# Output product of a hybrid decoder step on one Trainium2 core: squares summed apart, attention's rows tile by tile, no sums on GpSimd

## The chip, the cores and the metric

One of the eight cores of a Trainium2 chip (trn2) runs the whole program. The metric is device time in microseconds (us) of one execution. The engines are named PE (TensorE, matmuls; PEld is its weight load), DVE (VectorE), ACT (ScalarE), POOL (GpSimd) and SP (SyncE, which issues the weight DMAs).

## What is computed

Two layers of a decoder trunk, for 256 prompt tokens and 8 sample tokens together (T = 264 columns), in float32. Each layer is a SwiGLU block, a mixer and a second SwiGLU block, each behind an RMS norm:

```python
yp = yp + 0.5 * swiglu(rmsnorm(yp, norm_ffn1[l]), ...)
h = rmsnorm(yp, norm_mix[l])
b_g, u, qn, qp, ckv, kpe = mixer_project(h, ...)      # ckv = rmsnorm(kv_c), kpe = rope(k_pe)
conv_y = b_g * short_conv(u_hist, conv_w[l], SEQ)     # 512 wide
attn_o = prompt_mla(qn, qp, ckv, kpe, w_kv_b[l])      # 8 heads x 64 = 512 wide
merged = concatenate([rmsnorm(conv_y, gn_conv), rmsnorm(attn_o, gn_attn)])
yp = yp + merged @ w_o[l]                             # the output product, 1024 x 1024
yp = yp + 0.5 * swiglu(rmsnorm(yp, norm_ffn2[l]), ...)
```

## The kernel before, in words

Activations lie feature by feature: eight tiles of 128 features by 264 tokens. A weight arrives as a 1 MB chunk and is split into a high and a low part: ACT rounds it (line 231), DVE subtracts (line 233, "lo"), each in two halves of 128x512. A product is then three matmuls (lines 250 to 252: high by high, high by low, low by high). Five units (a column tile of 128 features each) fit in the split buffers, so the next unit is split when PE has finished an old one.

The code is traced in an order, and the scheduler then orders each engine's queue by its own model of readiness; each engine works through its queue strictly in that order. `behind()` puts the DVE half of a split behind the instruction that `after[0]` names at that moment. The mixer weaves three generators (`main`: the convolution's products; `prompt`: attention of the prompt; `sample`: attention of the sample) by the string ORDER.

`main` (lines 870 to 916): for each of the four convolution tiles, z is computed on DVE (line 901), ACT makes its scaled high part (905) and its square (907 or 910), DVE its low part (911) and the sum of squares in ssB (913). `h_out` (687) adds the squares of attention's rows into ssA on POOL (704). `latent` normalises the latents (578), rounds them on ACT (580), subtracts on DVE (581) and rotates the key on POOL (596 to 598).

The output product (933 to 987): `o_stats` (933) sums ssA and ssB over the features by a transposing reduction on DVE (316) and a matmul with `fold` (317, "sums"), then a reciprocal root in small DVE instructions (302 to 309, 939 to 945). `a_spread` (947) spreads the factor over rows (321) and, for each of attention's four tiles, multiplies (953, DVE), rounds (954, ACT) and subtracts (955, DVE); these are the tiles `qg` in the trace. `o_part` gives the matmuls of one k tile: k = 0 to 3 are the convolution's rows (`r` in the trace), k = 4 to 7 attention's. The first four output tiles are built side by side in four PSUM banks, k outermost; the last four one after another. `o_finish` scales a finished bank (963), adds it to y (964), lets a weight unit be split (`done`), and calls `finish_y`: the next block's high and low parts `xg` (331 ACT, 332 DVE), the square (336, 339 ACT) and its sum, on POOL for seven of eight tiles (343). The second SwiGLU then opens with four units at once, each one k tile behind the one before (`kouter`, lag 1), and takes the four PSUM banks over as `o_finish` frees them.

The scratch rows `wtile` share one tag, "w", with four buffers: the softmax rows p of a head (665), their transposed form (684), and the spread factors. Each stays taken from its first writer to its last reader. A softmax of head h can start when a buffer is free; `h_out` (694) frees two when it has used a pair of heads.

At the program's start the squares of y are summed at lines 1011 to 1022, tiles 1 to 3 on POOL, 5 to 7 on DVE.

Of the kernel before, what the change touches and what calls it, by code (L numbers as in the profile page):

```python
# [7 lines left out]
F32 = mybir.dt.float32  # L8
# [10 lines left out]
SEQ = 256  # L19
# [89 lines left out]
def trunk_kernel(ctx: ExitStack, tc: tile.TileContext, a: dict, o: dict):  # L109
# [199 lines left out]
        after[0] = V.scalar_tensor_tensor(r, t, 5.0, r, ALU.add, ALU.mult).ins  # L309
        return r  # L310

    def sums(ps, ss, c0=0):


        q = small(NBLK, tag="sums")
        V.tensor_reduce(q, ss.rearrange("p (c j) -> p c j", j=32), AX.X, ALU.add, apply_transpose=True)
        PE.matmul(ps[:, c0:c0 + NBLK], fold, q, start=True, stop=True)

    def over_rows(out, r):

# [8 lines left out]
    def finish_y(kt, g, split=True, square=True, pool=False, last=False):  # L329
        if split:  # L330
            S.activation(xg["h"][:, kt], y[:, kt], AF.Copy, scale=g)  # L331
            V.scalar_tensor_tensor(xg["l"][:, kt], y[:, kt], g, xg["h"][:, kt].bitcast(F32), ALU.mult, ALU.subtract)  # L332
        if not square:
            return
        if kt == 0:
            S.activation(ssA[:, :T], y[:, kt], AF.Square, scale=D ** -0.5)
        else:
            sq = t264()
            S.activation(sq[:, :T], y[:, kt], AF.Square, scale=D ** -0.5)
            if kt == KT - 1 and last:  # L340
                nrm["sq"] = sq
                return
            (G if pool else V).tensor_tensor(ssA[:, :T], ssA[:, :T], sq[:, :T], ALU.add)

    nrm = {}

# [149 lines left out]
    def mixer(l):  # L496
# [62 lines left out]
        kgs = [mt([P, 4, SEQ], f"kg{g}") for g in range(2)]  # L559
        qgs = [mt([P, 4, T], f"qg{g}") for g in range(2)]  # L560
        zh, zl = [], []
        Sc = Rb


# [9 lines left out]
        def latent():  # L574
            s2 = st["s2"]
            Rk = wtile(TP)
            over_rows(Rk, s2[:, 0:NBLK])
            V.tensor_tensor(ckvf, kvg, Rk[:, :T], ALU.mult)
            ckh, ckl = r264(), r264()
            S.activation(ckh, ckvf, AF.Copy)  # L580
            after[0] = V.tensor_tensor(ckl, ckvf, ckh.bitcast(F32), ALU.subtract).ins

            sel = small(8, tag="qsel")
# [9 lines left out]
            kp2 = t264()  # L593
            with behind():
                V.stream_shuffle(kp2[64:96, :T], kp1[64:96, :T], SWAP)
            G.tensor_tensor(kp1[64:96, :T], kp1[64:96, :T], cos[64:96], ALU.mult)
            G.tensor_tensor(kp2[64:96, :T], kp2[64:96, :T], sin[64:96], ALU.mult)
            G.tensor_tensor(kpf[64:96], kp1[64:96, :T], kp2[64:96, :T], ALU.add)

        def values():  # L600
            wh, wl = [w[:, 0, NH * NOPE:] for w in st["wkv"]]
# [85 lines left out]
        def h_out(t):  # L687
# [11 lines left out]
            if t == 0:  # L699
                S.activation(ssA[:, 0:SEQ], ps[:, 0:256], AF.Square, scale=CD ** -0.5)  # L700
            else:
                sq = t264()[:, :SEQ]
                S.activation(sq, ps[:, 0:256], AF.Square, scale=CD ** -0.5)
                G.tensor_tensor(ssA[:, 0:SEQ], ssA[:, 0:SEQ], sq, ALU.add)

        def prompt():
            low_rank()
# [162 lines left out]
        def main():  # L870
            cs, us = {}, {}
            for c in (0, 2):
                for part in (1, 2, 0):
                    for j in range(2):
# [24 lines left out]
                        else:  # L899
# [2 lines left out]
                            done()  # L902
                            g = gain("gn_conv", 4 * l, ct)
                            h, lo = r264(), r264()
                            S.activation(h, z, AF.Copy, scale=g)
                            if ct == 0:
                                S.activation(ssB[:, :T], z, AF.Square, scale=CD ** -0.5)
                            else:
                                sq = t264()[:, :T]
                                S.activation(sq, z, AF.Square, scale=CD ** -0.5)  # L910
                            V.scalar_tensor_tensor(lo, z, g, h.bitcast(F32), ALU.mult, ALU.subtract)
                            if ct:
                                V.tensor_tensor(ssB[:, :T], ssB[:, :T], sq, ALU.add)
                            zh.append(h)
                            zl.append(lo)
                        yield
# [16 lines left out]
        def o_stats():  # L933

            ps = bank("x")
            sums(ps, ssA)
            sums(ps, ssB, NBLK)
            v = small(2 * NBLK, tag="v2")
            V.tensor_scalar(v[:, 0:NBLK], ps[:, 0:NBLK], EPS, None, ALU.add)
            V.tensor_tensor(v[:, NBLK:], ps[:, NBLK:2 * NBLK], ev, ALU.add)  # L940
# [6 lines left out]
        def a_spread():  # L947
            fa = st["fa"]
            Ra = wtile(TP)
            over_rows(Ra, fa)  # L950
            for t in range(CT):
                f = t264()[:, :T]
                V.scalar_tensor_tensor(f, st["attn"][:, t], gain("gn_attn", 4 * l, t), Ra[:, :T], ALU.mult, ALU.mult)
                S.activation(mg[0][:, t], f, AF.Copy)
                V.tensor_tensor(mg[1][:, t], f, mg[0][:, t].bitcast(F32), ALU.subtract)

        def o_part(ps, w, k):
            xh, xl = (zh[k], zl[k]) if k < CT else (mg[0][:, k - CT], mg[1][:, k - CT])
# [10 lines left out]
        open_xg()  # L969
        us = [take() for _ in range(4)]  # L970
        pss = [bank("mm") for _ in range(4)]
        for k in range(KT):
            for w, ps in zip(us, pss):
                o_part(ps, w, k)
            if k == 2:
                a_spread()
            if k == 5:
                c_spread()
            if k == 5:
                c_store()  # L980
        for m in range(4):
            o_finish(m, pss[m])
        for m in range(4, KT):
            w, ps = take(), bank("mm")
# [27 lines left out]
    for kt in range(KT):  # L1012
        acc = hi if kt >= 4 else ssA[:, :T]
        if kt % 4 == 0:
            S.activation(acc, y[:, kt], AF.Square, scale=D ** -0.5)
        else:
            sq = t264()[:, :T]
            S.activation(sq, y[:, kt], AF.Square, scale=D ** -0.5)
            (V if kt >= 4 else G).tensor_tensor(acc, acc, sq, ALU.add)
        if kt == 3:  # L1020
            split_unit()
    V.tensor_tensor(ssA[:, :T], ssA[:, :T], hi, ALU.add)
# [129 lines left out]
```

## Time and profile before

| what | value |
| --- | --- |
| three runs | 1040.4, 1041.53, 1047.66 us; median 1041.53 |
| the profiled execution | 1033.67 us, its span 1031.9 us |
| mean granted TensorE clock of it | 0.995 |
| PE, DVE, ACT, POOL busy | 97%, 74%, 52%, 9% of the span |

The page's busy times are shares of the span; "idle before <-X" in a timeline row is how long the engine had waited before that instruction and whose work ended the wait. Starts of consecutive instructions on one engine may lie closer than their durations, since they are pipelined.

### The profile page before, as it was taken

The page shows a single profiled execution, that of the slowest core. Times are in us where ns is not written, and L with a number is a line of the kernel's source. Part 1 is how long each engine was busy: PE and PEld are TensorE (multiplying, and loading weights), DVE is VectorE, ACT ScalarE, POOL GpSimd, SP SyncE. Part 2 cuts the span into 40 slices and gives each one's busy share as a digit, 9 for nine tenths or more (in the row PEclk, how much of TensorE's full clock was granted, in tenths as well). Part 3 has the DMA queues.
Part 4 walks back from the last instruction along what each step waited for, and adds up shares of the span by engine and source line. Part 5 has one row for each costly group of instructions (what it writes and reads, how often), then busy time and mean ns, then how long its engine had stood idle before and what let it go on. Part 6 is the DMA issues. An engine that isn't in the chain of part 4 may idle for free.

```text
span 1031.9 us, 21616 instructions
## 1 busy us (share of the span) xinstructions
PE 1001.6 (97%) x8666; PEld 970.5 (94%) x8666; DVE 764.0 (74%) x1753; ACT 535.9 (52%) x1167; POOL 93.9 (9%) x135
## 2 busy tenths in 40 slices
PE   8999999999999999999999999999999899999996
PEld 7999999988788999999999999999878899999996
DVE  6988866689859877756688888566996897777452
ACT  6555445448636555545555555454674555555441
POOL 2110100030402000000001111000322100000000
PEclk9999999999999999999999999999999999999998
DMA  8867665535614755555566667454554265555531
GB/s 276 276 221 242 217 199 193 173 109 194 247 42 164 240 169 191 177 164 188 180 213 232 219 226 230 159 179 154 170 192 178 93 208 191 189 178 174 165 113 43
DMA packets 170787, 190.03 MB, mean 184 GB/s; under 512 B 3936, under 2 KB 163712, under 8 KB 170688
## 3 DMA queue, kind: packets, MB, share of 16 engines
q1 hardware_dynamic: 164048, 167.53, 49.7%
q0 software_dynamic: 5776, 19.49, 5.4%
q10 hardware_dynamic: 864, 1.64, 0.5%
q8 instruction: 68, 1.11, 0.4%
q14 instruction: 31, 0.25, 0.1%
HBM read 187.19 MB, written 1.49 MB: 183 GB/s over the span
## 4 chain that ended last, share of the span: by engine, by line
PE 85%; DVE 10%; ACT 3%; issue 1%; DMA 1%; ACTq 0%; SPq 0%; DVEq 0%
PE mm L250 27%; PE mm L252 27%; PE mm L251 26%; DVE lo L233 4%; PE x L779 1%; DVE y L964 1%; ACT hi L231 1%; DVE xg L332 1%; PE x L830 1%; DMA raw<-in_w_ffn_gate_dram 1%; PE x L694 1%; PE x L681 1%; DVE t L963 1%; ACT qg L635 0%; PE s L658 0%
## 5 line engine op out<-in xcount | busy, mean ns | idle before, releaser
L231 ACT ACTIVATE hi<-raw 128x512 fp32r<-128x512 f32 (+1 forms) x648 | 366.2, 612 | 367.3 <-PE mm L251 245.4
L233 DVE TENSOR_TENSOR lo<-raw,hi 128x512 fp32r<-128x512 f32 (+1 forms) x648 | 417.2, 677 | 112.2 <-ACT hi L231 102.7
L252 PE MATMUL mm<-xg,lo 128*128 128x264 f32 x1648 | 468.0, 284 | 7.1 <-DVE lo L233 7.0
L250 PE MATMUL mm<-xg,hi 128*128 128x264 f32 x1648 | 471.2, 286 | 2.4 <-DVE t L963 1.7
L251 PE MATMUL mm<-xg,hi 128*128 128x264 f32 x1648 | 467.4, 284 | 0.0
L252 PEld LDWEIGHTS mm<-xg,lo 128*128 128x128 f32 x1648 | 308.8, 188 | 10.6 <-DVE lo L233 9.6
L250 PEld LDWEIGHTS mm<-xg,hi 128*128 128x128 f32 x1648 | 310.5, 188 | 5.1 <-ACT hi L231 3.6
L251 PEld LDWEIGHTS mm<-xg,hi 128*128 128x128 f32 x1648 | 310.6, 188 | 0.2
L250 PE MATMUL mm<-act,hi 128*128 128x264 f32 x704 | 200.4, 285 | 0.0
L252 PE MATMUL mm<-act,lo 128*128 128x264 f32 x704 | 199.7, 284 | 0.0
L251 PE MATMUL mm<-act,hi 128*128 128x264 f32 x704 | 199.2, 283 | 0.0
L250 PEld LDWEIGHTS mm<-act,hi 128*128 128x128 f32 x704 | 132.3, 188 | 0.2 <-ACT t L1040 0.2
L252 PEld LDWEIGHTS mm<-act,lo 128*128 128x128 f32 x704 | 132.5, 188 | 0.0
L251 PEld LDWEIGHTS mm<-act,hi 128*128 128x128 f32 x704 | 132.4, 188 | 0.0
L464 POOL DMA_INDIRECT nat<-in_cache_ckv_dram,idx x32 | 33.4, 1044 | 445.7 <-DVE lo L233 189.7
L403 DVE TENSOR_TENSOR t<-mm,t 128x264 f32<-128x264 f32 x88 | 37.6, 427 | 40.1 <-PE mm L252 39.6
L394 DVE TENSOR_TENSOR t<-mm,Rw 128x264 f32<-128x264 f32 x88 | 37.6, 428 | 38.4 <-PE mm L252 38.4
L331 ACT ACTIVATE xg<-y,gains 128x264 fp32r<-128x264 f32 x48 | 24.1, 514 | 29.8 <-DVE y L449 19.1
L397 ACT ACTIVATE t<-t 128x264 f32<-128x264 f32 x88 | 36.3, 412 | 4.4 <-DVE t L394 4.3
L399 DVE SCALAR_TENSOR_TENSOR t<-t,t 128x264 f32<-128x264 f32 x88 | 37.6, 428 | 1.1 <-ACT t L397 1.1
L406 DVE TENSOR_TENSOR act<-t,act 128x264 fp32r<-128x264 f32 x88 | 37.7, 428 | 0.0
L405 ACT ACTIVATE act<-t 128x264 fp32r<-128x264 f32 x88 | 36.0, 409 | 0.7 <-DVE t L403 0.6
(230 smaller groups left out, 808.3 us busy)
## 6 DMA issues: line engine op xcount, KB each, us to landing
raw<-in_w_ffn_up_dram SPq DMA_DIRECT2D x44, 1024.0 KB, 5.2
raw<-in_w_ffn_gate_dram SPq DMA_DIRECT2D x43, 1024.0 KB, 5.2
raw<-in_w_ffn_down_dram SPq DMA_DIRECT2D x32, 1024.0 KB, 5.3
raw<-in_w_in_dram SPq DMA_DIRECT2D x14, 1024.0 KB, 5.4
raw<-in_w_ffn_down_dram SPq DMA_DIRECT2D x16, 768.0 KB, 4.6
raw<-in_w_o_dram SPq DMA_DIRECT2D x8, 1024.0 KB, 5.2
raw<-in_w_q_dram SPq DMA_DIRECT2D x2, 768.0 KB, 5.0
raw<-in_w_in_dram SPq DMA_DIRECT2D x2, 640.0 KB, 4.0
```

The source lines that it names most:

```text
L231: S.activation(h[:, k, f], raw[:, k, lo:hi][:, :, f], AF.Copy)
L233: V.tensor_tensor(r[:, k, f], raw[:, k, lo:hi][:, :, f], h[:, k, f].bitcast(F32), ALU.subtract)
L250: PE.matmul(ps, wh, xh, start=start, stop=False)
L251: PE.matmul(ps, wh, xl, start=False, stop=False)
L252: return PE.matmul(ps, wl, xh, start=False, stop=stop)
L394: V.tensor_tensor(g1, ps[:, :T], Rb, ALU.mult)
L397: S.activation(th, g1, AF.Tanh, scale=0.5)
L399: evac[0] = V.scalar_tensor_tensor(a1[m], th, 1.0, g1, ALU.add, ALU.mult).ins
L403: V.tensor_tensor(t, ps[:, :T], a1.pop(m), ALU.mult)
L405: S.activation(ah[:, m], t, AF.Copy)
L406: evac[0] = V.tensor_tensor(al[:, m], t, ah[:, m].bitcast(F32), ALU.subtract).ins
L464: G.indirect_dma_start(dst, None, src, bass.IndirectOffsetOnAxis(ap=idx[l][:, b:b + 1], axis=0))
```

## The change

In the order of the code: `sums` can continue an accumulation in PSUM. All sums of squares go to DVE (finish_y, h_out, the start). The latents are rounded by DVE straight from the product that makes them, no longer by ACT from the stored tile, and the rotated key is made by DVE. The last convolution tile's square is made by DVE into a tile of its own, `sqB`, taken from the "w" buffers early in the mixer, and summed by a matmul of its own; its low part is traced after that. `a_spread` multiplies all four tiles before it subtracts, and sets `after[0]`. The output product's first four tiles take the convolution's rows side by side and then attention's rows tile by tile.

```diff
-    def sums(ps, ss, c0=0):
+    def sums(ps, ss, c0=0, start=True, stop=True):
-        PE.matmul(ps[:, c0:c0 + NBLK], fold, q, start=True, stop=True)
+        PE.matmul(ps[:, c0:c0 + NBLK], fold, q, start=start, stop=stop)
...
-            (G if pool else V).tensor_tensor(ssA[:, :T], ssA[:, :T], sq[:, :T], ALU.add)
+            V.tensor_tensor(ssA[:, :T], ssA[:, :T], sq[:, :T], ALU.add)
...
+        sqB = wtile(TP)
+        G.memset(sqB[:, T:TP], 0.0)
...
+            ckh, ckl = r264(), r264()
+            V.tensor_tensor(ckh, kvg, Rk[:, :T], ALU.mult)
             V.tensor_tensor(ckvf, kvg, Rk[:, :T], ALU.mult)
-            ckh, ckl = r264(), r264()
-            S.activation(ckh, ckvf, AF.Copy)
...
-            G.tensor_tensor(kp1[64:96, :T], kp1[64:96, :T], cos[64:96], ALU.mult)
-            G.tensor_tensor(kp2[64:96, :T], kp2[64:96, :T], sin[64:96], ALU.mult)
-            G.tensor_tensor(kpf[64:96], kp1[64:96, :T], kp2[64:96, :T], ALU.add)
+                V.tensor_tensor(kp1[64:96, :T], kp1[64:96, :T], cos[64:96], ALU.mult)
+                V.tensor_tensor(kp2[64:96, :T], kp2[64:96, :T], sin[64:96], ALU.mult)
+                V.tensor_tensor(kpf[64:96], kp1[64:96, :T], kp2[64:96, :T], ALU.add)
...
-                G.tensor_tensor(ssA[:, 0:SEQ], ssA[:, 0:SEQ], sq, ALU.add)
+                V.tensor_tensor(ssA[:, 0:SEQ], ssA[:, 0:SEQ], sq, ALU.add)
...
+                            if ct < CT - 1:
...
+                            else:
+                                V.scalar_tensor_tensor(sqB[:, :T], z, 1.0 / CD, z, ALU.mult, ALU.mult)
+                                S.activation(h, z, AF.Copy, scale=g)
+                                st["lo"] = lo, z, g, h
...
             sums(ps, ssA)
-            sums(ps, ssB, NBLK)
+            sums(ps, sqB, NBLK, start=True, stop=False)
+            lo, z, g, h = st["lo"]
+            V.scalar_tensor_tensor(lo, z, g, h.bitcast(F32), ALU.mult, ALU.subtract)
+            sums(ps, ssB, NBLK, start=False, stop=True)
...
+            fs = []
             for t in range(CT):
-                f = t264()[:, :T]
-                V.scalar_tensor_tensor(f, st["attn"][:, t], gain("gn_attn", 4 * l, t), Ra[:, :T], ALU.mult, ALU.mult)
-                S.activation(mg[0][:, t], f, AF.Copy)
-                V.tensor_tensor(mg[1][:, t], f, mg[0][:, t].bitcast(F32), ALU.subtract)
+                fs.append(t264()[:, :T])
+                after[0] = V.scalar_tensor_tensor(fs[t], st["attn"][:, t], gain("gn_attn", 4 * l, t), Ra[:, :T], ALU.mult, ALU.mult).ins
+                S.activation(mg[0][:, t], fs[t], AF.Copy)
+            for t in range(CT):
+                V.tensor_tensor(mg[1][:, t], fs[t], mg[0][:, t].bitcast(F32), ALU.subtract)
...
-        for k in range(KT):
+        for k in range(CT):
             for w, ps in zip(us, pss):
                 o_part(ps, w, k)
-            if k == 2:
+            if k == 1:
                 a_spread()
-            if k == 5:
                 c_spread()
-            if k == 5:
                 c_store()
         for m in range(4):
+            for k in range(CT, KT):
+                o_part(pss[m], us[m], k)
             o_finish(m, pss[m])
...
-            (V if kt >= 4 else G).tensor_tensor(acc, acc, sq, ALU.add)
+            V.tensor_tensor(acc, acc, sq, ALU.add)
```

## Rows read from the trace of the kernel before

**Rows 1.** The page: the chain that ended last, shares of the span by engine.
```profile
PE 85%; DVE 10%; ACT 3%; issue 1%; DMA 1%; ACTq 0%; SPq 0%; DVEq 0%
```

**Rows 2.** Windows: stretch, its us, busy of each engine (instructions), granted clock, DMA.
```profile
260.00:290.00 30.00, 29.82 (x512) 22.48 (x508) 23.27 (x88) 18.13 (x58) 12.21 (x17) 1.00 0.60 213
...
300.40:308.10 7.70, 7.63 (x48) 7.48 (x49) 3.08 (x9) 2.21 (x6) 0.00 (x0) 0.78 0.01 2
...
795.20:803.70 8.50, 6.59 (x54) 6.27 (x52) 6.44 (x23) 2.30 (x6) 0.00 (x0) 1.00 0.35 118
803.70:809.90 6.20, 6.14 (x48) 5.99 (x49) 3.10 (x9) 2.24 (x6) 0.00 (x0) 1.00 0.01 3
809.90:821.60 11.70, 11.70 (x98) 11.70 (x97) 11.70 (x23) 10.29 (x23) 3.73 (x4) 1.00 0.53 170
821.60:836.50 14.90, 12.95 (x100) 12.19 (x99) 13.57 (x34) 6.78 (x15) 1.82 (x3) 1.00 0.45 149
```

**Rows 3.** Timeline of PE, layer 1: start, us, line, tiles, idle before.
```profile
798.09 0.28 PE L251 MATMUL mm<-r,hi 128*128 128x264 f32 x1
...
798.52 0.37 PE L252 MATMUL mm<-r,lo 128*128 128x264 f32 x1
...
801.50 0.29 PE L252 MATMUL mm<-r,lo 128*128 128x264 f32 x1
803.75 0.75 PE L250 MATMUL mm<-qg,hi 128*128 128x264 f32 x4 [1.96 <-ACT qg L954]
...
824.55 0.36 PE L250 MATMUL mm<-xg,hi 128*128 128x264 f32 x1 [0.83 <-DVE t L963]
...
828.25 0.51 PE L252 MATMUL mm<-xg,lo 128*128 128x264 f32 x2 [1.09 <-DVE lo L233]
```

**Rows 4.** Timeline of DVE, layer 1, from the last convolution tile to attention's tiles.
```profile
795.39 0.43 DVE L901 TENSOR_TENSOR t<-t,mm 128x264 f32<-128x264 f32 x1 [0.23 <-PE mm L252]
796.86 0.49 DVE L911 SCALAR_TENSOR_TENSOR r<-t,gains,r 128x264 fp32r<-128x264 f32 x1 [1.04 <-ACT r L905]
...
797.73 0.48 DVE L316 TRANSPOSE_TENSOR_REDUCE sm<-ssB 128x9 f32<-128x288 f32 x1
798.70 0.17 DVE L939 TENSOR_SCALAR sm<-x 128x9 f32<-128x9 f32 x1 [0.48 <-PE x L317]
...
801.20 0.68 DVE L233 TENSOR_TENSOR lo<-raw,hi 128x512 fp32r<-128x512 f32 x1
...
802.76 1.29 DVE L953 SCALAR_TENSOR_TENSOR t<-attn,gains,w 128x264 f32<-128x264 f32 x3
```

**Rows 5.** Timeline, layer 1: additions to y on DVE, and one sum on POOL.
```profile
809.73 0.77 DVE L964 TENSOR_TENSOR y<-y,t 128x264 f32<-128x264 f32 x2
...
815.29 0.99 DVE L964 TENSOR_TENSOR y<-y,t 128x264 f32<-128x264 f32 x1
...
815.03 0.96 POOL L343 TENSOR_TENSOR ssA<-ssA,t 128x264 f32<-128x264 f32 x1 [1.90 <-ACT t L339]
```

**Rows 6.** Timeline of DVE, the program's start.
```profile
13.88 2.31 DVE L233 TENSOR_TENSOR lo<-raw,hi 128x512 fp32r<-128x512 f32 x2 [0.86 <-ACT hi L231]
```

**Rows 7.** Timeline, layer 1: the latents on DVE, the rotated key on POOL.
```profile
725.03 0.43 DVE L581 TENSOR_TENSOR r<-ckvf,r 128x264 fp32r<-128x264 f32 x1 [0.80 <-ACT r L580]
...
725.98 3.05 DVE L233 TENSOR_TENSOR lo<-raw,hi 128x512 fp32r<-128x512 f32 x4
...
727.32 1.16 POOL L596 TENSOR_TENSOR t<-t,con 32x264 f32<-32x264 f32 x1
```

**Rows 8.** Timeline, layer 1: softmax rows and their use in attention of the prompt.
```profile
770.17 0.35 DVE L665 CUSTOM_DVE_ANT_0 w<-s,tri,sm 128x128 f32<-128x128 f32 x1 [0.15 <-PE x L694]
...
775.01 0.55 DVE L684 COPY w<-x 128x384 f32<-128x384 f32 x1
...
786.28 0.87 PE L694 MATMUL x<-w,v 128*64 128x256 f32 x8
...
789.12 0.87 PE L694 MATMUL x<-w,v 128*64 128x256 f32 x8
```

More of the change, by code (lines that the diff above doesn't have):

```diff
@@ L904, in main @@
                             h, lo = r264(), r264()
-                            S.activation(h, z, AF.Copy, scale=g)
-                            if ct == 0:
-                                S.activation(ssB[:, :T], z, AF.Square, scale=CD ** -0.5)
-                            else:
[L909 to L913, printed above, removed]
+                            if ct < CT - 1:
+                                S.activation(h, z, AF.Copy, scale=g)
+                                if ct == 0:
+                                    S.activation(ssB[:, :T], z, AF.Square, scale=CD ** -0.5)
+                                else:
+                                    sq = t264()[:, :T]
+                                    S.activation(sq, z, AF.Square, scale=CD ** -0.5)
+                                V.scalar_tensor_tensor(lo, z, g, h.bitcast(F32), ALU.mult, ALU.subtract)
+                                if ct:
+                                    V.tensor_tensor(ssB[:, :T], ssB[:, :T], sq, ALU.add)
+                            else:
+                                V.scalar_tensor_tensor(sqB[:, :T], z, 1.0 / CD, z, ALU.mult, ALU.mult)
+                                S.activation(h, z, AF.Copy, scale=g)
+                                st["lo"] = lo, z, g, h
                             zh.append(h)
@@ L936, in o_stats @@
             sums(ps, ssA)
-            sums(ps, ssB, NBLK)
+            sums(ps, sqB, NBLK, start=True, stop=False)
+            lo, z, g, h = st["lo"]
+            V.scalar_tensor_tensor(lo, z, g, h.bitcast(F32), ALU.mult, ALU.subtract)
+            sums(ps, ssB, NBLK, start=False, stop=True)
             v = small(2 * NBLK, tag="v2")
```

## The prediction

> **What bounds the kernel now.** I began with the chain of work that ended last [rows 1]: 85% of it is PE, 10% VectorE. So the kernel is bound by matmuls, and an edit can only give back places where PE waits or runs slowly. The windows over the stages [rows 2] show where those are. The reader should compare instruction counts with lengths. Where PE is fed, 98 matmuls take 11.70 us, 0.119 each (809.9 to 821.6). The stretch before it has 48 in 6.20 us, nearly as dense. But the same 48 in layer 0 (300.4 to 308.1) take 7.70 us, and there the granted clock reads 0.78 instead of 1.00. The opening of the second SwiGLU has 100 in 14.90 us, where 100 x 0.119 = 11.9 would do: 3.0 us of waits. The convolution's rows of the output product take 8.50 us for 54 instructions. Attention (260 to 290) keeps PE busy for 29.82 of 30 us: nothing to win there, only to lose. Each of these stretches occurs twice, once per layer, with equal lengths but for the clock.
>
> The timeline of PE [rows 3] shows the waits themselves: the last convolution row starts at 801.50, attention's first at 803.75, behind ACT's rounding of its rows; then two waits at 824.55 and 828.25, behind VectorE's evacuation of a bank and behind the low part of a weight. VectorE explains the latter [rows 2]: it works 3.10 of 6.20 us while four banks fill side by side, then 11.70 of 11.70 us, and the backlog still stands when the SwiGLU opens.
>
> **Term 1, the wait before attention's rows.** Before: 803.75 - 801.50 = 2.25, less one spacing of 0.12, so 2.1 us per layer. On VectorE [rows 4] z starts at 795.39, waits for ACT (1.04 us before the low part at 796.86), the sum goes into ssB, the reduction starts at 797.73 and the first result from PE is used at 798.70, 0.97 later. New: z 0.43, square 0.49 (a like form at 796.86), then again 0.97: 795.39 + 1.89 = 797.3, 1.4 us earlier, as long as the older sums are reduced before z or behind sqB. If the low part and the other reduction come in between, 0.97 - 0.48 = 0.5 us remains. Then from 801.20 to 802.76 two weight splits (0.68 the first) and the spreading stand in front of attention's tiles; the new `after[0]` puts the splits behind: 1.56 less the spreading's 0.48 (a like form at 797.73), another 1.1 us. Attention's first tile thus starts at about 802.76 - 2.5 = 800.3, its rounded rows reach PE 0.99 later (802.76 to 803.75), at 801.3, before PE is through. The low part now comes after four multiplications (1.29 / 3 = 0.43 each): 800.3 + 1.7 + 0.4 = 802.4. PE has the third sums to do first; one costs the step from 798.09 to 798.52 less 0.12, so 0.31 [rows 3], and four high products bring it to about 802.4. I leave 0.2 of waiting and 0.3 of sums: gain 1.6 us per layer. Bounds: 0 (nothing shorter comes through) to 2.0.
>
> **Term 2, the opening of the SwiGLU.** Output tiles finished one by one let VectorE begin after 12 matmuls (1.4 us) instead of after nearly all 48: most of its 3.1 idle us are used [rows 2]. Against that, two splits (1.1 us) now lie behind attention's tiles, where they used to lie ahead. The sums on POOL: six per layer. Two additions on VectorE take 0.77 us together, 0.39 each; one that meets a POOL sum takes 0.99 [rows 5], 0.6 more. Six moved sums cost 6 x 0.39 = 2.3, and free about 6 x 0.5 to 0.6 = 3.0 to 3.6 us (not each meets an addition in full). So VectorE gains roughly 3.1 - 1.1 + 0.7 = 2.7 us or a little more on PE, against 3.0 us of waits. What will be late next is the chain of the last unit: its buffers come free only with the last output tile, and it has to be split by ACT and VectorE before 828.25's matmul can run. I leave 0.6 us: gain 2.4 per layer. Bounds: 0, if VectorE's queue is as late as before, to 3.0. No queue is held by a moved sum unless ACT's square is late. ACT is busy 10.3 of 11.7 us there [rows 2], so it can be, and the evacuations would queue behind; that is in the 0.6.
>
> [...]
>
> **Term 3, the clock.** [...] With the wait gone I take 1.5 as gained. Bounds: -1.5 (a new wait drops it elsewhere) to 1.5. [...]
>
> **Term 4, the start.** Two splits take 2.31 us beside POOL's three sums [rows 6], where one split alone takes 0.68 [rows 4]: 0.9 us or more is lost. Three additions on VectorE cost 1.2, and 0.86 of idle time lies ahead of them. Gain 0.5; bounds -0.5 to 1.0.
>
> **Term 5, the latents.** VectorE waited 0.80 us for ACT's rounding at 725.03 [rows 7]; one product of 0.43 replaces it, 0.4 earlier. Three instructions for the rotated key come onto VectorE, some 1.3 us, ahead of the splits that PE needs; but the four splits there took 3.05 us, 0.76 each instead of at most 0.68 [rows 4], beside POOL's version. That is -0.4 + 1.3 - 0.3 = 0.6 later at first, which I expect the later splits, free of POOL, to give back: 0. Bounds: 0.8 us per layer either way. The three sums of `h_out` (1.2 us of VectorE, 23.27 of 30 us busy in that stretch) I cost at nothing; attention's PE queue hides them.
>
> **Term 6, the buffer.** sqB takes one of four "w" buffers from its clearing on POOL, early in the mixer, until the statistics. Attention's softmax rows have three left. Already before, a softmax waited for a buffer: at 770.17, for the output of the first pair [rows 8]. With three, the second head of each pair has to wait too. The last pair came 2.8 us behind the third (786.28 to 789.12) since head 7 had been prepared. Without that it needs a whole chain: 770.17 to 775.01, plus the copy of 0.55 and the product's 0.87, 6.3 us; so attention would end 3.5 us later per layer. Its sums were reduced before z came, and the convolution's chain still follows, so most of that is covered: I take 0.5 per layer. Bounds: 0 to 3.5.
>
> **The sum**, against the profiled execution's 1033.67 us: 2 x 1.6 + 2 x 2.4 + 1.5 + 0.5 + 0 - 2 x 0.5 = 9.0 us. That gives 1024.7. The median of the three runs lies 7.9 us above the profiled execution, so I take the difference off the median: 1041.5 - 9.0 = 1032.5 us.
>
> **The rivals.** A is the forecast: 0.42, with 6 to 10.4 us gained.
>
> B: the buffer costs nothing and both waits go almost wholly: 2 x 1.8 + 2 x 2.8 + 1.5 + 0.6 = 11.3, 1030.2 us. For it: attention's chain has slack; four rounds of 6.3 us from 770.2 would be done at the same time as now. Against: the last unit's split. 0.34.
>
> C: the change does not do what it says in the queue. The scheduler already mixes the four banks (four high products at 803.75 in one row [rows 3]), and VectorE has as much to do as before; then banks still finish late, and term 2 is nothing: 9.0 - 4.8 = 4.2, 1037.3 us. For it: VectorE full for 11.7 of 11.7 us. Against: those 3.1 idle us. 0.16.
>
> D, on the other side: attention starves for buffers. If the planner runs out of convolution products before attention is through, two rounds of 6.3 us lie bare, and the 48 convolution rows (5.7 us) can cover only part: 6.9 per layer, 13.8 in all, against 9.0 + 1.0 gained elsewhere: 1041.5 + 3.8 = 1045.3 us. It decides from 5.0 us per layer on. For it: PE is full there and a buffer was waited for with four. Against: the rounds fit on paper. 0.08.
>
> **How the numbers follow.** A measurement of this kernel can tell about 1%, 10.4 us, from no change. B alone is beyond that: faster 0.34. A, C and a part of D (0.03) lie within: 0.61. Slower by over 1% needs more than D's price: 0.05. The range: at the low end B's with all bounds of terms 1 to 4 in favour, 2 x 2.0 + 2 x 3.0 + 1.5 + 1.0 = 12.5, so 1029, less 3 for the spread of the runs (1040.4 to 1047.7): 1026. At the high end C with term 6 at half its bound, 1037.3 + 2 x 1.7 = 1041, and a little: 1042. For the likeliest case alone it is 1031 to 1036.
>
> **What would show it.** Right: PE's step from the last convolution row to the first `qg` row under 0.6 us; the stretch after it at 6 us and clock 1.00 in both layers; the first bank's evacuation (963) some 1.5 us after the first `qg` row; additions at 964 all near 0.42; the SwiGLU's opening with at most 1 us of waits. Wrong: a `qg` row that waits for 955; PE idle behind 674 or 684 in attention, or convolution products running out before the last 694 (D); evacuations still late behind sums at 343 (C); the first splits behind the latents later than before by more than 0.8 us (term 5).

## The result and the profile after

The kernel after takes 1035.44 us (median of 7 runs, 1034.67 to 1035.76), the kernel before on the same chip 1043.08 (7 runs, 1040.40 to 1048.99): ratio 0.9926, 95% interval 0.9905 to 0.9947. So 7.6 us are gained, where 9.0 were forecast; the interval leaves out 1, so the gain is clear of the scatter. Yet the profiled executions stand the other way round: after 1035.27 (span 1033.5), before 1033.67 (span 1031.9). The profile of before belongs to an execution 6.7 us below the lowest of its ordinary runs; the experiments show why.

The page of after: span, busy engines, and the chain that ended last by engine.
```profile
span 1033.5 us, 21623 instructions
...
PE 1005.3 (97%) x8670; PEld 974.2 (94%) x8670; DVE 766.1 (74%) x1784; ACT 534.1 (52%) x1163; POOL 72.4 (7%) x110
...
PE 88%; DVE 6%; ACT 2%; issue 1%; DMA 1%; ACTq 0%; SPq 0%; DVEq 0%
```
VectorE has gone from 10 to 6% of the chain [rows 1]. The wait before attention's rows, on PE's timeline of after, layer 1:
```profile
807.27 0.29 PE L252 MATMUL mm<-r,lo 128*128 128x264 f32 x1
808.22 0.75 PE L250 MATMUL mm<-qg,hi 128*128 128x264 f32 x4 [0.67 <-ACT qg L966]
809.33 0.39 PE L251 MATMUL mm<-qg,hi 128*128 128x264 f32 x1 [0.36 <-DVE qg L968]
```
The step is 0.95 us instead of 2.25 [rows 3], and a second wait, for the first low part, follows. On VectorE the same place answers to [rows 4]:
```profile
801.08 0.43 DVE L903 TENSOR_TENSOR t<-t,mm 128x264 f32<-128x264 f32 x1 [0.33 <-PE mm L252]
801.54 0.43 DVE L919 SCALAR_TENSOR_TENSOR w<-t 128x264 f32<-128x264 f32 x1
802.01 0.48 DVE L316 TRANSPOSE_TENSOR_REDUCE sm<-w 128x9 f32<-128x288 f32 x1
802.55 0.49 DVE L947 SCALAR_TENSOR_TENSOR r<-t,gains,r 128x264 fp32r<-128x264 f32 x1
802.96 0.47 DVE L316 TRANSPOSE_TENSOR_REDUCE sm<-ssB 128x9 f32<-128x288 f32 x1
804.09 0.17 DVE L950 TENSOR_SCALAR sm<-x 128x9 f32<-128x9 f32 x1 [0.66 <-PE x L317]
```
From z to the first result are 3.01 us, against 3.31 before: the low part (L947) and the other reduction lie between. The windows of after over the output product of layer 1 and the opening of its SwiGLU answer to the last three of [rows 2]:
```profile
808.20:814.40 6.20, 5.82 (x45) 5.61 (x46) 6.13 (x15) 4.55 (x10) 0.00 (x0) 1.00 0.01 3
814.40:826.40 12.00, 12.00 (x101) 12.00 (x100) 12.00 (x29) 8.93 (x20) 0.00 (x0) 1.00 0.53 175
826.40:841.00 14.60, 14.60 (x123) 14.60 (x122) 12.78 (x35) 8.34 (x18) 0.00 (x0) 1.00 0.48 152
```
In the opening PE works 14.60 of 14.60 us, with 123 matmuls where 100 stood in 14.90. VectorE works 6.13 of 6.20 us in the stretch where it worked 3.10. In layer 0 the stretch behind the first `qg` row, which read a granted clock of 0.78 before, now reads 1.00:
```profile
305.20:311.40 6.20, 5.76 (x45) 5.55 (x46) 6.13 (x15) 4.55 (x11) 0.00 (x0) 1.00 0.01 3
```

And one thing that nobody had forecast, in attention: the list of PE's waits in after begins with
```profile
PE x L814 <- issue: 7.9, 10, 1.2
PE mm L250 <- ACT hi L231: 2.9, 2, 1.6
PE mm L252 <- DVE lo L233: 2.6, 4, 1.0
```
L814 (L812 before) is the scatter that turns the sampled softmax rows with 128 tiny matmuls per layer. "issue" means that the engine waited for nothing that the profile shows.

For all runs the span is cut at four kinds of places in PE's timeline: the first matmul of line 526 in each layer, the first convolution row of the output product (`mm<-r`), the first `mm<-qg` row, and the first SwiGLU matmul behind it. The table sums both layers, in us. Chips of two kinds were met, told apart by the kernel before: on the first it takes 1040 to 1049 us, on the second 1033 to 1040. The chip of the profile "before, as shown" isn't on record; its time and its stages are those of the second kind. Each row is one profiled execution; ordinary runs of the same kernel scatter around it, by 2 us for e2 and by 6 to 7 for before on the second kind.

| kernel (chip) | up to L526 | L526 to conv. rows | conv. rows | rest of output product | SwiGLUs | span |
|---|---|---|---|---|---|---|
| before, as shown | 213.5 | 157.7 | 17.1 | 37.2 | 606.3 | 1031.9 |
| before again, e1 (second) | 215.1 | 159.8 | 17.1 | 37.1 | 605.9 | 1035.0 |
| before a third time, e9 (second) | 214.7 | 158.0 | 17.1 | 37.0 | 606.3 | 1033.0 |
| after (first) | 212.8 | 169.5 | 14.7 | 36.5 | 600.1 | 1033.5 |
| after, e5 and e11 (first) | 212.7 | 169.5, 169.7 | 14.7 | 36.5 | 600.1 | 1033.5, 1033.7 |
| after, k outermost, e3 (second) | 212.8 | 157.6 | 14.7 | 36.5 | 601.6 | 1023.1 |
| after, own buffer, e2 (second) | 212.7 | 154.6 | 13.5 | 36.5 | 600.1 | 1017.4 |
| after, sums on POOL, e6 (first) | 212.8 | 168.8 | 14.7 | 36.5 | 601.8 | 1034.6 |
| before, sums on VectorE, e7 (first) | 213.8 | 169.5 | 17.1 | 37.0 | 601.3 | 1038.7 |
| own buffer, shorter chain, e8 (first) | 212.8 | 167.4 | 13.0 | 36.5 | 600.2 | 1030.0 |
| after, no gathers, e12 (first) | 212.8 | 155.4 | 14.7 | 36.5 | 600.1 | 1019.5 |

Outside the second column after is 10.1 us shorter than before (0.7 + 2.4 + 0.7 + 6.2, with the roundings). In the second column it is 11.7 us longer.

### The profile page after: what moved, and what is told of

Its sections match the earlier page's. It is cut to its first block, busy times and chain, and to the rows that moved or that the text cites. A ratio compares the mean times of both kernels' runs of the same rounds, so it can differ in the third digit from the quotient of the medians.

```text
span 1033.5 us, 21623 instructions
## 1 busy us (share of the span) xinstructions
PE 1005.3 (97%) x8670; PEld 974.2 (94%) x8670; DVE 766.1 (74%) x1784; ACT 534.1 (52%) x1163; POOL 72.4 (7%) x110
## 3 DMA queue, kind: packets, MB, share of 16 engines
q8 instruction: 68, 1.11, 0.4%
## 4 chain that ended last, share of the span: by engine, by line
PE 88%; DVE 6%; ACT 2%; issue 1%; DMA 1%; ACTq 0%; SPq 0%; DVEq 0%
PE mm L250 28%; PE mm L252 27%; PE mm L251 27%; DVE lo L233 2%; PE x L781 1%; PE x L696 1%; ACT hi L231 1%; PE x L832 1%; DMA raw<-in_w_ffn_gate_dram 1%; PE x L683 1%; DMA raw<-in_w_in_dram 1%; PE x L814 0%; PE s L660 0%; DVE t L965 0%; ACT qg L637 0%
## 5 line engine op out<-in xcount | busy, mean ns | idle before, releaser
L233 DVE TENSOR_TENSOR lo<-raw,hi 128x512 fp32r<-128x512 f32 (+1 forms) x648 | 413.0, 671 | 112.3 <-ACT hi L231 102.7
L250 PE MATMUL mm<-xg,hi 128*128 128x264 f32 x1648 | 472.1, 287 | 3.0 <-ACT hi L231 2.9
L250 PEld LDWEIGHTS mm<-xg,hi 128*128 128x128 f32 x1648 | 311.4, 189 | 5.4 <-ACT hi L231 3.6
L250 PE MATMUL mm<-act,hi 128*128 128x264 f32 x704 | 200.4, 285 | 0.0
L250 PEld LDWEIGHTS mm<-act,hi 128*128 128x128 f32 x704 | 132.3, 188 | 0.2 <-ACT t L1053 0.2
L464 POOL DMA_INDIRECT nat<-in_cache_ckv_dram,idx x32 | 33.6, 1050 | 483.9 <-DVE lo L233 228.3
```

What stands on the lines that cost most here:

```text
L233: V.tensor_tensor(r[:, k, f], raw[:, k, lo:hi][:, :, f], h[:, k, f].bitcast(F32), ALU.subtract)
L250: PE.matmul(ps, wh, xh, start=start, stop=False)
L464: G.indirect_dma_start(dst, None, src, bass.IndirectOffsetOnAxis(ap=idx[l][:, b:b + 1], axis=0))
```

## The experiments

### Where attention lost 12 us: the kernels unchanged (e1, e5, e9, e11)

No edit. The first question was whether the change brought the waits at L814.

> The kernel before, unchanged, profiled once more. Theory S (the starved scatter of attention's turn belongs to ordinary runs of both kernels, and the first profile of before was one that escaped it): this execution takes about 1040 to 1047 us; its attention stage, from the first L526 matmul to the first convolution row, takes 84 to 86 us in layer 0 instead of 78.4, with rows of some us of 'PE x L812 <- issue' and a clock that falls behind them. Rival C (the change brought the starvation, by its buffer or by the new order of the queue): the stage again takes 78.4 and 79.4 us, no issue waits at L812, and the 8 us that ordinary runs take more than the first profile lie in the output stage or in the SwiGLU.

Before took 1035.05 us here (12 runs, 1033.21 to 1037.52): a chip of the second kind. The stage took 79.5 and 80.3 us with no issue wait at L812. That looks like rival C. But on the same chip the kernels of e2 and e3 had none either, and e3 has, up to the output product, PE's queue of after instruction by instruction. So the kernel after itself was run again.

> The kernel after, unchanged, once more. TensorE's queue up to the output product is the same, instruction by instruction, in this kernel and in the two runs that showed no issue waits at the turn's scatter (k outermost; no gathers, but for the name of the operand). Theory S' (the starved scatter hangs on where and when the execution took place, not on the program): no or few issue waits at L814, attention stage 78 to 79.5 us in both layers, about 1022 to 1024 us where before takes 1035 to 1036. Rival P (it hangs on the program as it is laid out in memory, for which a few instructions more or less are enough): issue waits of 10 us and more at L814 again, the stage at 84 to 85 us, 1033 to 1036 us, the same in every run.

1035.16 us against 1044.08 for before (ratio 0.9912, 0.9880 to 0.9943), stage 84.2 and 85.2, 7.9 us of issue waits at L814. That is what rival P expects; but it was a chip of the first kind, so it leaves open whether program or chip decides.

> The kernel before, unchanged, profiled again. So far chips of two kinds have been met: one on which the kernel before takes 1040 to 1049 us, and one on which it takes 1033 to 1040. Theory S on a chip of the first kind: its profile has issue waits of 8 us or more in attention, in the scatter at L812 or beside it, on other engines too; a clock of 0.5 to 0.9 behind them; an attention stage of 83 to 87 us instead of 78 to 80. Rival: the stage takes 78 to 80 us there too and the difference between the chips lies elsewhere. On a chip of the second kind the stage is 78 to 80.5 us and nothing is told apart.

1037.17 us, stage 78.5 and 79.5: the second kind again, and nothing told apart, as the expectation says.

> The kernel after, unchanged. On a chip of the second kind (before 1033 to 1040 us), where it has not been timed yet: theory S'' (the starved scatter belongs to chips of the first kind, whatever the kernel) gives no issue waits at L814, an attention stage of 78 to 79.5 us and 1022 to 1024 us, ratio about 0.988, so more than the 0.992 of the first kind; rival P (the program of after starves everywhere) gives 1033 to 1036 us again. On a chip of the first kind: 1035 us, stage 84 to 85 us, as twice before.

1035.44 us against 1044.43, ratio 0.9921 (0.9890 to 0.9952): the first kind, stage 84.3 and 85.4. So unchanged and with a profile, before was seen on the second kind and after on the first alone. What decides is e7 below: on a first-kind chip a kernel with before's code in attention has a stage of 169.5 us, like after. The list of PE's waits in e7:
```profile
PE x L681 <- DVE sm L766: 2.6, 1, 2.6
PE x L681 <- issue: 2.6, 1, 2.6
...
PE x L812 <- issue: 1.8, 3, 1.2
```
And e3, with after's attention, has 157.6 on the second kind, as before's three profiles have 157.7 to 159.8. The loss goes with the chip, not with the change: 11.8 us for before's attention (169.53 - 157.74, e7 against before as shown), 11.8 for after's (169.44 - 157.61, after against e3), and 12.9 for e2's (167.44 - 154.58, e8 against e2). No kernel with the gathers was profiled on both kinds, so rival P is held off by these three pairs of nearly equal programs, and by the ordinary runs of one and the same program: before takes 1043 to 1044 us on the first kind and 1035 to 1037 on the second (medians).

### What starves the scatter: the gathers left out (e4, e10, e12)

The kernel leaves out eight gathers per layer and reads a buffer that is there anyway.
```diff
-            nat = keep.tile([P, 4, NSLOT, KV], F32, tag="B", bufs=2, name=nm("nat"))
-            for b in range(4):
-                gather(nat[:, b].rearrange("p t c -> p (t c)"), "cache_ckv", l, 4 * s + b)
+            nat = Bset[s]
...
-                    PE.matmul(..., nat[:, b, t], ...)
+                    PE.matmul(..., nat[:, b, t % 5, 0:KV], ...)
```


> The kernel after without the eight gathers of latents per layer: attention's sampled values are taken from a buffer that is already there, so that part of the result is left out. Theory S in the form 'DMA': the scatter of the turn starves because the gathers and the weight loads fill the DMA engines, which also bring the instructions; without the gathers the issue waits at L814 go (16.7 us in all in after), and the attention stage falls to 78 to 80 us, so 1023 to 1027 us. Rival F (the instructions come late whatever the transfers, for the turn's many small matmuls run faster than they can be brought): issue waits stay above 8 us and the time within 3 us of after.

1021.32 us (4 runs) beside 1035.82 for before, stage 77.7 in both layers. It agrees with theory S, but shows nothing: this chip was of the second kind, where nothing starves with gathers either (e3).

> The kernel after without the eight gathers of latents per layer (attention's sampled values come from a buffer that is already there: that part of the result is left out), as once before on the chip where nothing starved. On a chip of the first kind, where after takes 1035 us: theory 'DMA' (the instructions come late because the gathers fill the DMA engines) gives an attention stage of 77.5 to 79 us without issue waits at L814, and about 1021 to 1023 us, as on the other chip. Rival F (the chip brings instructions late whatever the transfers) leaves the stage at 83 to 85 us and the time at 1032 to 1035. On a chip of the second kind it gives 1021 us again and tells nothing.

1021.39 us, on the second kind again: nothing told apart.

> The kernel after without the eight gathers of latents per layer (attention's sampled values come from a buffer that is already there: that part of the result is left out). On a chip of the first kind: theory 'DMA' gives no issue waits at L814, an attention stage of 77.5 to 79 us and 1021 to 1023 us; rival F leaves the stage at 83 to 85 us and the time at 1032 to 1035. On a chip of the second kind: 1021 us, as twice before; then beside the kernel after on the same chip it gives what the gathers cost where nothing starves, which both theories put at 0 to 3 us.

Now on a first-kind chip, beside after's 1035.44: 1021.30 us (4 runs, 1021.22 to 1021.58), stage 77.69 in both layers, no issue wait at the scatter. Time and stage are those of theory "DMA", and F falls: the gathers bring the loss. That they do it by keeping instructions back isn't shown by this; the last section comes to it. Without gathers the two kinds of chip agree to 0.1 us. The windows show the stretch; columns as in [rows 2]. After, first kind:
```profile
267.00:273.00 6.00, 1.95 (x37) 1.54 (x37) 1.30 (x5) 1.79 (x7) 4.00 (x6) 0.92 1.01 398
273.00:279.00 6.00, 5.93 (x61) 4.82 (x61) 3.79 (x18) 2.53 (x7) 0.00 (x0) 0.51 0.53 215
```
Without gathers, first kind:
```profile
267.00:273.00 6.00, 6.00 (x109) 5.21 (x108) 5.68 (x26) 5.34 (x19) 0.23 (x2) 1.00 0.02 5
273.00:279.00 6.00, 6.00 (x189) 4.87 (x191) 5.41 (x19) 3.39 (x11) 1.28 (x3) 1.00 0.53 174
```
With gathers, second kind (e3):
```profile
267.00:273.00 6.00, 6.00 (x107) 5.19 (x107) 5.48 (x26) 5.16 (x19) 3.99 (x6) 1.00 1.00 385
273.00:279.00 6.00, 5.91 (x172) 4.48 (x174) 5.58 (x19) 3.50 (x11) 1.30 (x3) 1.00 0.98 368
```
The DMA engines are full (1.01 and 1.00) in the first and the third alike. Only on the first kind do PE, VectorE and ACT come nearly to a stand beside them: 37 matmuls instead of 107. Behind the stretch in which PE worked 1.95 of 6 us the granted clock reads 0.51 over the next six us, where the other two runs read 1.00; part of the loss, by estimate from that, falls there.

### What emptied the opening of the SwiGLU (e3, e6, e7)

Two edits answer for the same wait. Each was taken away alone, and one was made alone. e3 puts k outermost again:
```diff
-        for k in range(CT):
+        for k in range(KT):
             for w, ps in zip(us, pss):
                 o_part(ps, w, k)
...
-            for k in range(CT, KT):
-                o_part(pss[m], us[m], k)
```


> The kernel after, but attention's rows of the output product go over all four banks for each k again, with k outermost, instead of bank by bank; squares, splits and sums stay as in after. Theory T (the finishing bank by bank lets VectorE begin early and is what empties the opening of the SwiGLU): the first evacuation comes back to some 5.5 us after the first qg row, the SwiGLU opening has about 2 us of waits again, 1.5 to 3 us per layer, so 1039 to 1041. Rival U (VectorE was slow because of POOL's sums; with them moved the order of the banks is worth little): under 0.5 us per layer, 1035 to 1036.

The first evacuation comes back to 802.74, 5.65 us behind the first `qg` row, as theory T has it, and VectorE idles 2.37 us ahead of it; e3, layer 1:
```profile
802.74 0.80 DVE L976 TENSOR_TENSOR t<-mm,Rw 128x264 f32<-128x264 f32 x2 [2.37 <-PE mm L252]
```
Yet the opening has only 0.3 us of waits on the evacuation (`mm L250 <- DVE t L976`) in either layer. The SwiGLU column is 601.6 against 600.1: with the sums moved, the order of the banks is worth 0.75 us per layer. The time of 1024.24 us (ratio 0.9884 on this chip) is not to be held against the expected 1035 to 1041, which came from a chip of the first kind.

e6 gives the six sums per layer back to GpSimd:
```diff
-            V.tensor_tensor(ssA[:, :T], ssA[:, :T], sq[:, :T], ALU.add)
+            (G if pool else V).tensor_tensor(ssA[:, :T], ssA[:, :T], sq[:, :T], ALU.add)
```


> The kernel after with the six sums of squares per layer in the output product's finishing (L343) back on GpSimd; bank by bank as in after. Theory U (POOL's sums slowed VectorE, and moving them emptied the opening of the SwiGLU; finishing bank by bank gave 0.7 us per layer): the opening gets about 2 to 2.4 us of waits back per layer, so 4 to 5 us more than the kernel after on this chip. Rival T (with the banks finished one by one VectorE has enough slack even beside POOL): under 0.6 us per layer, within 1.2 us of after.

1037.32 us (8 runs) beside after's 1035.16 on the same chip: 2.2 us by the medians, 1.1 by the spans. On VectorE additions and on POOL sums collide again as in [rows 5]; e6, layer 1, additions to y:
```profile
817.00 0.42 DVE L977 TENSOR_TENSOR y<-y,t 128x264 f32<-128x264 f32 x1
818.68 0.98 DVE L977 TENSOR_TENSOR y<-y,t 128x264 f32<-128x264 f32 x1
```
and the sum beside the second:
```profile
818.42 0.95 POOL L343 TENSOR_TENSOR ssA<-ssA,t 128x264 f32<-128x264 f32 x1 [1.90 <-ACT t L339]
```
PE's wait comes back (`mm L250 <- DVE t L976`, 0.7 and 0.6 us), and the SwiGLU column grows by 1.7. Nearer to rival T, but more than its 1.2 by the medians.

e7 makes this edit alone, in the kernel before (the two lines of e6's diff exchanged).

> The kernel before with one part of the change alone: the six sums of squares per layer at L343 on VectorE. Theory U: this part alone gives 2 to 2.4 us per layer in the opening of the SwiGLU, so 4 to 5 us in all, ratio about 0.9955. Rival T: VectorE has as much to do as before while k is outermost and the splits lie ahead of attention's tiles; under 1 us in all.

1039.87 us beside 1044.08, ratio 0.9950 (0.9930 to 0.9970), so 4.2 us; the SwiGLU column falls from 606.3 to 601.3. That is theory U's 4 to 5 us.

Taken together: the sums alone give 5.0 of the SwiGLU column's 6.2 us (e7); without them, the rest of the change gives 4.4 (e6); without the order of the banks, 4.7 (e3). So the sums and the rest are substitutes: each fills most of the same 3 us per layer, and added up they would be counted twice. What in the rest does it, the order of the banks or the splits' new place behind attention's tiles, was not parted.

### The buffer, and a version that beats both (e2, e8)

e2 leaves four `w` buffers to attention and puts the last square where a key tile is dead:
```diff
-        sqB = wtile(TP)
-        G.memset(sqB[:, T:TP], 0.0)
...
+                                sqB = st["sqB"] = mt([P, 4, SEQ], "kg0").rearrange("p h t -> p (h t)")[:, 0:TP]
+                                G.memset(sqB[:, T:TP], 0.0)
...
-            sums(ps, sqB, NBLK, start=True, stop=False)
+            sums(ps, st["sqB"], NBLK, start=True, stop=False)
```


> The kernel after, but the square of the last tile lies in the space of a key tile that is free by then, so that attention keeps all four 'w' buffers until its end. Theory S: the buffer has nothing to do with the starvation; the attention stage stays at 84 to 86 us and the time within 1 us of after's 1035.4. Rival C in its form 'the buffer': the stage goes back to 78.4 and 79.4 us, and the time falls by 8 to 11 us, to about 1026. The prediction's term 6 put the buffer at 1.0 us over both layers (0 to 7).

1020.69 us (4 runs), ratio 0.9853 (0.9837 to 0.9869) on the second kind. As the starvation was absent from this chip, the run doesn't decide between S and C; beside e3 it does price the buffer, though not closely. In the second column it is 154.6 against 157.6: 3.0 us. But that is one execution of each, of e2 the fastest of four runs (1019.13) and of e3 the slowest (1024.89). By the medians e2 is 3.6 us faster, of which the convolution rows (1.2) and the SwiGLU column (1.5), taken as profiled, leave 0.8 for the buffer; e8 below against after gives the same 0.8 on the first kind (2.4 us by the medians, convolution rows 1.7 shorter, SwiGLU column 0.15 longer). So 0.8 to 3.0 us over both layers. The last pair of heads shows where it comes from. Softmax rows of the last heads on VectorE, layer 1, e2 with four buffers:
```profile
773.85 0.35 DVE L665 CUSTOM_DVE_ANT_0 w<-mm,tri,sm 128x128 f32<-128x128 f32 x1
```
PE's products of the third and fourth pair, e2:
```profile
776.41 0.87 PE L694 MATMUL x<-w,v 128*64 128x256 f32 x8
779.26 0.87 PE L694 MATMUL x<-w,v 128*64 128x256 f32 x8
```
The same softmax rows in e3, with three buffers:
```profile
780.25 0.35 DVE L667 CUSTOM_DVE_ANT_0 w<-mm,tri,sm 128x128 f32<-128x128 f32 x1 [0.20 <-PE x L683]
```
PE's third and fourth pair, e3:
```profile
780.03 0.87 PE L696 MATMUL x<-w,v 128*64 128x256 f32 x8
782.79 0.65 PE L696 MATMUL x<-w,v 128*64 128x256 f32 x2
784.46 0.86 PE L696 MATMUL x<-w,v 128*64 128x256 f32 x6
```
With four buffers the last head's softmax starts 2.6 us before the third pair's product; with three, only once that product has begun, and the fourth pair is torn in two.

The convolution rows take 13.5 instead of 14.7 in e2. There the low part came behind both reductions, though it is written ahead of the second, and the first result was used 2.39 us after z instead of 3.01; VectorE in e2, layer 1:
```profile
785.57 0.43 DVE L901 TENSOR_TENSOR t<-t,mm 128x264 f32<-128x264 f32 x1 [0.32 <-PE mm L252]
...
786.50 0.48 DVE L316 TRANSPOSE_TENSOR_REDUCE sm<-kg 128x9 f32<-128x288 f32 x1
786.90 0.44 DVE L316 TRANSPOSE_TENSOR_REDUCE sm<-ssB 128x9 f32<-128x288 f32 x1
787.26 0.45 DVE L947 SCALAR_TENSOR_TENSOR r<-t,gains,r 128x264 fp32r<-128x264 f32 x1
787.96 0.17 DVE L950 TENSOR_SCALAR sm<-x 128x9 f32<-128x9 f32 x1 [0.25 <-PE x L317]
```
e8 fixes that order on purpose, and puts the convolution's spreading behind attention's tiles too:
```diff
+            sums(ps, ssB, NBLK, start=False, stop=True)
             lo, z, g, h = st["lo"]
-            V.scalar_tensor_tensor(lo, z, g, h.bitcast(F32), ALU.mult, ALU.subtract)
-            sums(ps, ssB, NBLK, start=False, stop=True)
+            after[0] = V.scalar_tensor_tensor(lo, z, g, h.bitcast(F32), ALU.mult, ALU.subtract).ins
...
-                c_spread()
+                with behind():
+                    c_spread()
```


> The kernel after with the last square in the key tile's space (as in the run with its own buffer), and two instructions taken out of the chain to attention's rows: the last tile's low part goes behind both reductions, and the spreading of the convolution's scale behind attention's four multiplications. Theory: the chain's two pieces cost 0.36 and 0.4 us, of which PE still waited 0.2 to 0.6 us per layer, so 0.5 to 1.1 us in all off the 1020.7 of the run with its own buffer. Rival: the first convolution row of the last tile then waits for the low part, or the first evacuation for the scale; no gain or up to 1 us worse.

It fell on the first kind: 1032.78 us beside after's 1035.16 and before's 1044.08 (ratio 0.9884, 0.9853 to 0.9915). The convolution rows take 13.0 us, 0.5 less than e2's. This version beats both kernels on that chip; starvation still takes its part (second column 167.4). The expected 0.5 to 1.1 us off e2 can't be read from the times, since the two ran on chips of different kinds; the convolution rows give 0.45 over both layers, just under its lower end.

## Why the prediction was right, and where not

The time (1035.4 for 1032.5, inside 1026 to 1042 and inside the likeliest case's 1031 to 1036) and the sign came out; so did a size under the 1% that the text took for the least that can be told from nothing (0.74%); the interval of 0.9905 to 0.9947 shows that less than 1% could be told here. Rival A was the case that happened. By steps:

**Term 1**, 1.6 us per layer forecast. Measured: the convolution rows 1.22 shorter, the rest of the output product 0.40 longer by the wait for the low part, so 0.8. The step that failed: "1.4 us earlier, as long as the older sums are reduced before z or behind sqB". The low part and a reduction came in between, for which the text had 0.5 ready, and 0.3 came. Where only the reduction does (e2), the term is 1.83 - 0.40 = 1.4. Two of the text's own signs say the same: the step to the first `qg` row is 0.95 us and not under 0.6, and the wait for a low part (955 before, 968 after), named there as a sign of being wrong, came with 0.36 us.

**Term 2**, 2.4 per layer: measured 2.9 and 3.2, the whole of the waits. Right in its mechanism (additions at 0.42 to 0.43 throughout), too low in size. The "chain of the last unit", for which 0.6 was left, was not late. The working added both edits up in one sum; e7 and e6 show that the moved sums alone give 5.0 of the 6.2, and all the rest without them 4.4. The first evacuation came at 810.97, 2.75 us behind the first `qg` row and not 1.5: VectorE had attention's low parts and a split to do first, and it cost nothing. On VectorE an evacuation of 0.43 us is followed 0.35 us after its start, so ahead of its end, by the next instruction:
```profile
810.97 0.43 DVE L976 TENSOR_TENSOR t<-mm,Rw 128x264 f32<-128x264 f32 x1
811.32 0.68 DVE L233 TENSOR_TENSOR lo<-raw,hi 128x512 fp32r<-128x512 f32 x1
```

**Term 3**, 1.5: right. It is the 7.70 us of layer 0 less the 6.20 of layer 1 [rows 2]. The stretch behind attention's rows takes 18.27 us in layer 0 and 18.26 in layer 1 of after. In all four profiles with the old wait (before, e1, e9, e7) layer 0 is 1.3 to 1.5 us longer than layer 1. So in the output product the loss came once in each of the four, in layer 0; why never in layer 1 was not shown. At the program's start the clock of the same kernel varied: before keeps 1.00 there in the profile shown, and reads 0.50 for 3.4 us from 20.4 in e1 and from 18.7 in e9.

**Term 4**, 0.5: measured 0.75 against before as shown. Against e1 (2.3) and e9 (1.9) it looks larger, since in these two the clock fell at the start, as just told; in no profile with the change did it. Two splits now take 1.28 us instead of 2.31 [rows 6], and PE waits 1.2 us in all for low parts there instead of 1.9.

**Terms 5 and 6**, 0 and -1.0: by the profiles together nothing (157.7 to 157.6, before as shown against e3), but of two parts that cancel. The buffer costs 0.8 us over both layers by the medians and 3.0 by the profiles (e2 against e3), by the very mechanism described, "the second head of each pair has to wait"; whether the forecast 1.0, and with it "most of that is covered", holds is thus open. The other edits in this stage (latents, rotated key, the sums of `h_out`) gave 3.2 by the profiles (157.7 to 154.6), where the text had costed them at nothing; its "nothing to win there", read from PE's 29.82 busy of 30 us, is the step that failed. Latents account for 0.5 us per layer, the distance from L526 to the value product at L606 (9.22 before, 8.75 in after); how the rest divides was not tried. D needed 6.9 us per layer and fell. C fell too: the opening has no waits.

The sum thus was 10.2 for 9.0 by the profiles without starvation. That it came so near is luck in part: over both layers term 1 was forecast 1.6 too large, term 2 1.4 and terms 5 and 6 1.1 too small. On the first kind the gain is 7.6 to 9.0 by three pairs of medians. After itself was never timed on the second kind; e3's 1024.24 less the 1.5 of its SwiGLU column puts it near 1022.7 by estimate, beside 1035.8 for before. That would be 13 us and not 10.2, since the profile of before (1033.67) lies near the fastest of its runs there, and it would be beyond the 1%, on case B's side. So that A's size came out hangs also on the kind of chip that the result was measured on.

What the prediction could not see is the step "I take the difference off the median": the profile came from an execution without the starvation that before's code has on the chip of its ordinary runs. The 7.9 us between profile and median were named but not explained. It did no harm because the attention of both kernels loses alike (11.8 us by the pairs above). Why before scatters over 9 us there and after over 3 (1034.67 to 1037.44) stays open: there is no profile of the unchanged kernel before on that kind.

## What to carry to other kernels

When the profiled execution is faster than every ordinary run, ask first what that execution escaped, and profile again before trusting its stages. Two remedies for one wait are substitutes: price each alone, and give the wait away only once. A scratch tile borrowed from a rotating pool costs whatever its last free slot was hiding; a tile that is dead by then (e2) is worth looking for. A stage's length in one profiled execution can be off by 2 us, as before's three show here (157.7 to 159.8); put the medians of ordinary runs beside it before pricing an edit.

## What the runs showed of the hardware that was not expected

On one kind of chip PE, VectorE and ACT came nearly to a stand beside full DMA engines (after: busy 1.95, 1.30 and 1.79 of 6 us, DMA 1.01), and on another they didn't (e3: 6.00, 5.48 and 5.16 of 6 us, DMA 1.00). In after on the first kind, PE's timeline while gathers fill the DMA:
```profile
267.89 0.35 PE L814 MATMUL x<-con,ws 128*32 128x32 f32 x16
268.79 0.20 PE L814 MATMUL x<-con,ws 128*32 128x32 f32 x1 [0.55 <-issue]
270.21 0.25 PE L814 MATMUL x<-con,ws 128*32 128x32 f32 x3 [1.21 <-issue]
271.64 0.25 PE L814 MATMUL x<-con,ws 128*32 128x32 f32 x4 [1.18 <-issue]
273.07 0.67 PE L814 MATMUL x<-con,ws 128*32 128x32 f32 x30 [1.18 <-issue]
```
After 16 matmuls in a row they come by ones, threes and fours, up to 1.43 us apart. VectorE and ACT show the same in that stretch (their busy time falls to 1.30 and 1.79 of 6 us). In e8 it shows in another place: ACT stands idle for 5.48 us up to 271.57, and PE waits 3.99 us for ACT, with no issue wait of its own. The DMA view of after for 266 to 272 us shows what the DMA engines carried:
```profile
DMA packets 645, 2.36 MB, mean 393 GB/s; under 512 B 69, under 2 KB 69, under 8 KB 645
...
q0 software_dynamic: 645, 2.36, 99.9%
```
All 645 packets are the gathers'; none is of an instruction queue, while the run without gathers (e12) has one each there:
```profile
q8 instruction: 1, 0.02, 0.9%
q14 instruction: 1, 0.01, 0.4%
```
Over the whole execution the page of after has 68 packets and 1.11 MB on q8, 16.3 KB each, and 32 packets and 0.26 MB on q14, 8.1 KB each; other instruction queues don't appear on it.

So it is tempting to read the standstill as engines without instructions, whose transfers queue behind the gathers'. That is the author's guess, and the packets speak against it as the whole answer. PE's 8670 matmuls and 8670 weight loads are 255 to each packet of q8; that q8 is PE's queue is the author's estimate from these counts, and was not shown. Ahead of the standstill the packets of q8 start at 250.0 and 265.3 us in after and at 250.0 and 265.4 in e3, those of q14 at 225.2 and 233.9 in both. The next ones come at 271.5 (q14) and 273.4 (q8) in e3, at 275.8 and 276.8 in after. So up to 271.5 us e3, on the second kind, had no more instruction packets than after, under as full a DMA; its DMA view for 266.6 to 271.4 us:
```profile
q0 software_dynamic: 498, 1.81, 98.4%
```
Yet its engines worked on, as the windows show. e3:
```profile
268.20:271.50 3.30, 3.30 (x68) 2.75 (x56) 3.30 (x19) 2.46 (x8) 2.65 (x3) 1.00 1.01 385
```
After:
```profile
268.20:271.50 3.30, 0.50 (x6) 0.35 (x5) 0.43 (x1) 0.59 (x2) 2.63 (x3) 1.00 1.01 398
```
The later packets of after can follow from the standstill as well as cause it.

What holds the engines up thus stays open. e12 takes away, with the transfers, also their issuing by GpSimd (L464, 1.05 us each on the page of after), and the two were not parted. What the runs show is that leaving out the gathers takes 14.1 us off after on the first kind (1035.44 to 1021.30), and that another chip of the same type runs the same queue under the same DMA load without a stall. What sets the two kinds of chip apart was not found.
